# Two weighted sums in the choice of experts: each list laid out four times over by ScalarE ahead of the product

## The chip, the core and the metric

One Trainium2 chip, one of its cores. The time is what the device takes for one execution of the whole kernel, in microseconds; shown is the median of several executions.

## What is computed

One layer of a network for two groups of tokens, 128 of a prompt and 1024 latent ones, with a width of 1024. After two token mixers (a gated one and a recurrent one) comes a channel mixer that picks, for each token and each of 8 heads, 16 out of 16384 small experts. This part of the reference matters here:

```python
v1, i1 = lax.top_k(s[:, :, 0], PEER_TOPK)
v2, i2 = lax.top_k(s[:, :, 1], PEER_TOPK)
cand = (v1[..., :, None] + v2[..., None, :]).reshape(n_tok, PEER_HEADS, PEER_TOPK * PEER_TOPK)
cand_idx = (i1[..., :, None] * N_KEYS + i2[..., None, :]).reshape(...)
top_v, top_j = lax.top_k(cand, PEER_TOPK)
idx = jnp.take_along_axis(cand_idx, top_j, axis=-1).reshape(n_tok, PEER_HEADS * PEER_TOPK)
g = jax.nn.softmax(top_v, axis=-1)
```

Two lists of 128 keys are scored, the best 16 of each are kept, the 256 sums of pairs are searched for the best 16, and the pair of key indices behind each winner names its expert. Each token's output is the sum, over its 128 experts, of gelu(x . u) g v.

## The kernel before

Tokens lie on the partitions, 128 to a tile; tile 0 is the prompt, tiles 1 to 8 the latent tokens. The kernel goes through the prompt, then through the recurrent mixer of all latent tiles, then through the group of tiles 5 to 8 (GA), then that of tiles 1 to 4 (GB), each with its weights read as units of 512 KB. A unit is split by `split` (lines 98 to 100) into a rounded part, which ScalarE copies (line 99), and a rest, which VectorE subtracts (line 100); TensorE multiplies with both (`mmx`, lines 124 to 131). The experts are then applied in two ways. For tiles 4 to 8 (`DENSE`) a table G of gates is built with one-hot products (`build_G`, lines 515 to 560) and a loop over all 128 blocks of 128 experts (lines 1055 to 1081) multiplies everything: this is the dense loop, which takes the second half of the time. For tiles 0 to 3 (`GATHER`) the rows of the chosen experts are fetched one by one by GpSimd's indirect DMAs, and VectorE does the dot products and the sums (`gather`, lines 792 to 827).

The choice for a tile is `combine` (lines 422 to 513). `top16` has left the best 16 values `tv` and indices `ti` of both key lists. Of the 256 sums only 50 can be among the best 16; they are written to `cand` (lines 434 to 440), and `top16` finds the best 16 of each head among them (lines 443 to 446), values in `cv`, places in `cp`. `itf` and `pf` are the indices and places in half precision. The place is turned into two key indices without a lookup: `cmp_` compares each place with the starts of the 16 rows of sums (line 466), `di` holds the differences of neighbouring indices of the first list (lines 468 and 469), and the sum over `cmp_` times `di` is the index (line 470 and `tree`, lines 461 to 465). A second such sum, with the lengths of the rows (line 476), gives the place within the row, and a third, a comparison for equality (line 481) times the indices of the second list (line 482), gives the second index. Each product has 8 heads x 16 x 16 = 2048 elements a partition in half precision, winner innermost: in lines 470 and 482 the second factor has one value of the list for each run of 16 (`lp`, line 458), in line 476 it is a constant table that lies in full. Line 488 is an exponential on ScalarE, for the gates.

`combine` is a generator: each `yield` is a place where other work may come between. It runs for tile 0 ahead of the latent tokens, for tiles 5 to 8 while GB's first units are worked on (`choose_q`, advanced by `tick` with the rates of line 34 and 642), for tile 4 in two halves of four heads each at the end of GB (lines 736 to 741 and 763), and for tiles 1 to 3 inside the dense loop (`combine_late`, lines 767 to 782, advanced by `fill`, line 1013), where its lists lie in row buffers and VectorE's instructions are recorded under line 119. The order of each engine's instructions is fixed when the program is built, by a planner that takes the program's order as priority and estimated durations; at run time each engine does its instructions in that order and waits for others by semaphores.

Of the kernel before, what the change touches and what calls it, by code (L numbers as in the profile page):

```python
# [11 lines left out]
F16 = mybir.dt.float16  # L12
# [3 lines left out]
AF = mybir.ActivationFunctionType  # L16
OP = mybir.AluOpType
# [19 lines left out]
NC_ = 50  # L37
# [14 lines left out]
def hybrid_kernel(ctx, tc, x_all, pos, c2t, w_ada, b_ada, wst, wspt, bsp, lbraw, vecs, fng, skt, state,  # L52
                  ut, urow, vrow, masks, ident_d, small, y_p, y_s, ns):
    nc = tc.nc
    V, A, P, G = nc.vector, nc.scalar, nc.tensor, nc.gpsimd
# [366 lines left out]
    def combine(gp, t, tv, ti, al=None, c4=None, V=V, h0=0, h1=8, res=None):  # L422

        if al is None:
            def al(name, n, dt=F32):
                return gp.tile([128, n], dt, name=name, bufs=1)

            def c4(name):
                return gp.tile([128, 2048], F16, name=name, tag="c4", bufs=3)
        h8 = lambda x: x.rearrange("p (a b) -> p a b", a=8)[:, 0:nh]  # L430
        nh = h1 - h0
        tv, ti = tv[:, h0:h1], ti[:, h0:h1]
        hs = slice(h0 * 16, h1 * 16)
        cand = h8(al("cand", 8 * NC_))
        for i in range(8):
            n = LENS[i]
            V.tensor_tensor(out=cand[:, :, OFFS[i]:OFFS[i] + n], in0=tv[:, :, 1, 0:n],
                            in1=tv[:, :, 0, i:i + 1].to_broadcast([128, nh, n]), op=OP.add)
        V.tensor_tensor(out=cand[:, :, 42:50], in0=tv[:, :, 0, 8:16],
                        in1=tv[:, :, 1, 0:1].to_broadcast([128, nh, 8]), op=OP.add)  # L440
# [7 lines left out]
        itf = al("itf", 256, F16).rearrange("p (a b c) -> p a b c", a=8, b=2)[:, 0:nh]  # L448
# [6 lines left out]
        cmp_, prod = [c4(n).rearrange("p (a b c) -> p a b c", a=8, b=16)[:, 0:nh] for n in ("cmp", "prod")]  # L455
        SH = [128, nh, 16, 16]
        hk = lambda x: x[:, :, None, :].to_broadcast(SH)
        lp = lambda x: x[:, :, :, None].to_broadcast(SH)
        cst = lambda x: x[:, None].to_broadcast(SH)

        def tree(dst):
            for n in (8, 4, 2):
# [4 lines left out]
        di = h8(al("di", 128, F16))  # L467
        V.tensor_tensor(out=di[:, :, 0:15], in0=itf[:, :, 0, 1:16], in1=itf[:, :, 0, 0:15], op=OP.subtract)
        V.memset(di[:, :, 15:16], 0.0)
        V.tensor_tensor(out=prod, in0=cmp_, in1=lp(di), op=OP.mult)  # L470
        yield
        tree(r3(res[:, 0]))
        V.tensor_tensor(out=r3(res[:, 0]), in0=r3(res[:, 0]),
                        in1=itf[:, :, 0, 0:1].to_broadcast([128, nh, 16]), op=OP.add)
# [4 lines left out]
        V.tensor_tensor(out=pf, in0=pf, in1=ro, op=OP.subtract)  # L479
        yield  # L480
        V.tensor_tensor(out=cmp_, in0=hk(pf), in1=cst(C["cj"]), op=OP.is_equal)
        V.tensor_tensor(out=prod, in0=cmp_, in1=lp(itf[:, :, 1, :]), op=OP.mult)
        yield
        tree(r3(res[:, 1]))

# [76 lines left out]
    def group(gp, tiles, hpar, native):  # L562
# [172 lines left out]
        for b in range(16):  # L735
            if b == 8:
                for i in split_at:
                    res = gp.tile([128, 384], F32, name="res", bufs=1).rearrange("p (a b) -> p a b", a=3)
                    halves[i] = res
                    choose_q.append(combine(gp, tiles[i], tv[i], ti[i], h1=4, res=res))  # L740
                    rate["choose"] = 1.5
            w = unit(u + 44 + b, native)
            skb = gp.tile([128, 128], F32, name="skb", bufs=2)
            nc.sync.dma_start(skb, skt[:, b, :])
            ps = pmm("pq")
            projT(ps[:, :T], w, opd_q)
            qs = h512("qs")
            A.activation(qs[:, :T], ps[:, :T], AF.Copy)
            pss = ptp("psc")
            for i in range(n):  # L750
                P.matmul(pss[:, i * 128:(i + 1) * 128], qs[:, i * 128:(i + 1) * 128], skb, start=True, stop=True)
            for i in range(n):
                top16(gp, pss[:, i * 128:(i + 1) * 128], tv[i][:, b // 2, b % 2, :], ti[i][:, b // 2, b % 2, :], 128)
        rate["gather"] = before
        for i in range(n):
            t = tiles[i]
            if tiles is GB and t in GATHER:

                for z, x in enumerate((tv[i], ti[i].bitcast(F32))):
                    nc.sync.dma_start(tvi_d[t][:, z * 256:(z + 1) * 256], x.rearrange("p a b c -> p (a b c)"))  # L760
                late.append(t)
            elif i in halves:
                choose_q.append(combine(gp, t, tv[i], ti[i], h0=4, res=halves[i]))
            else:
                choose_q.append(combine(gp, t, tv[i], ti[i]))
# [289 lines left out]
    for e in range(129):  # L1055
        if e < 128:
# [6 lines left out]
            if e < 2:  # L1063
                a = early[e]
            else:
                a = dp.tile([128, TD], F32, name="a", bufs=2)
# [127 lines left out]
```

## Time and profile before

| | us |
|---|---|
| median of 3 runs | 3648.53 (3641.53 to 3650.37) |
| the profiled execution's own time | 3648.09 |
| its span, from the first to the last instruction | 3646.3 |
| TensorE, VectorE, ScalarE, GpSimd busy | 3339.6, 2834.4, 1109.9, 1432.2 |

PE is TensorE, PEld its weight loads, DVE VectorE, ACT ScalarE, POOL GpSimd, SP the engine that issues most DMAs. L99 is line 99 of the kernel before. A row such as `prod<-cmp,di 128x2048` names what is written and what is read; what stands in brackets is how long the engine sat idle ahead of the instruction, and what it waited for. The dense loop starts at about 1740 us and ends some 20 us before the span does.

### The profile page before, as it was taken

Reading aid. Unit: us, or ns where it says so; the run is one execution under the profiler, and the core shown is the slowest. Engines: PE = TensorE matmul, PEld = TensorE weight load, DVE = VectorE, ACT = ScalarE, POOL = GpSimd, SP = SyncE. Lnnn points to the kernel's source line nnn. Section 1 sums busy time; section 2 is a strip of 40 time slices with the busy share of each in tenths; the row PEclk is TensorE's granted clock in tenths of the full one; section 3 lists DMA queues with packets and bytes.
Section 4 is the critical chain, followed back from the end, with each engine's and each line's share of the span. In section 5 each row is a group of like instructions: output and inputs, shape, how many; then the busy total and the mean of one; then the engine's idle time right before and its main releaser. Section 6 shows DMA issues by size and latency. Waiting matters only on the chain. (4 is left out here: it accounts for less than half of the span.)

```text
span 3646.3 us, 48811 instructions
## 1 busy us (share of the span) xinstructions
PE 3339.6 (92%) x17547; PEld 2765.2 (76%) x17547; DVE 2834.4 (78%) x5427; ACT 1109.9 (30%) x2075; POOL 1432.2 (39%) x1128
## 2 busy tenths in 40 slices
PE   8888999899888899877789999989999989999997
PEld 4375888675666676566788988888898878898996
DVE  2316668786799888697787889888888888788887
ACT  2511343320323565625222222222222222222222
POOL 0102101654112323200365564655555466555654
PEclk9899999999989999999899999999999999999998
DMA  8787323799533778742898998899989799989986
GB/s 286 281 294 248 117 89 106 260 316 346 178 121 122 254 288 312 246 155 107 274 331 307 321 325 281 309 316 327 322 316 321 257 331 337 328 304 318 335 320 248
DMA packets 361956, 971.12 MB, mean 266 GB/s; under 512 B 32720, under 2 KB 142672, under 8 KB 356080
## 3 DMA queue, kind: packets, MB, share of 16 engines
q0 software_dynamic: 149824, 546.37, 42.3%
q1 hardware_dynamic: 211888, 421.62, 33.6%
q8 instruction: 138, 2.26, 0.3%
q14 instruction: 106, 0.87, 0.1%
HBM read 897.07 MB, written 70.80 MB: 265 GB/s over the span
## 5 line engine op out<-in xcount | busy, mean ns | idle before, releaser
L802 POOL DMA_INDIRECT gu<-in_urow_dram,ix x512 | 692.4, 1352 | 1039.5 <-DVE jk L805 465.3
L815 POOL DMA_INDIRECT gv<-in_vrow_dram,ix x512 | 685.4, 1339 | 783.1 <-DVE acc L820 384.5
L805 DVE SCALAR_TENSOR_TENSOR jk<-gu,h2r 128x1024 f16<-128x1024 f32 x512 | 625.5, 1222 | 139.1 <-DMA gu<-in_urow_dram,ix 132.4
L820 DVE SCALAR_TENSOR_TENSOR acc<-gv,act,acc 128x1024 f32<-128x1024 f32 x508 | 651.3, 1282 | 37.7 <-DMA gv<-in_vrow_dram,ix 30.1
L129 PE MATMUL pH<-h2DH,uH 128*128 128x320 f32 x2016 | 625.7, 310 | 10.9 <-DVE accd L1052 10.2
L131 PE MATMUL pH<-h2DH,uL 128*128 128x320 f32 x2016 | 623.4, 309 | 3.4 <-DVE uL L100 3.4
L130 PE MATMUL pH<-h2DL,uH 128*128 128x320 f32 x2016 | 623.8, 309 | 0.0
L129 PEld LDWEIGHTS pH<-h2DH,uH 128*128 128x128 f32 x2016 | 380.2, 189 | 21.0 <-DVE accd L1052 14.9
L130 PEld LDWEIGHTS pH<-h2DL,uH 128*128 128x128 f32 x2016 | 380.0, 188 | 4.5
L131 PEld LDWEIGHTS pH<-h2DH,uL 128*128 128x128 f32 x2016 | 379.8, 188 | 4.4 <-DVE uL L100 4.4
L129 PE MATMUL pout<-vH,aH 128*128 128x512 f32 x768 | 298.6, 393 | 23.3 <-ACT vH L99 16.1
L130 PE MATMUL pout<-vL,aH 128*128 128x512 f32 x768 | 300.2, 391 | 5.3 <-DVE vL L100 5.3
L99 ACT ACTIVATE vH<-vr 128x1024 fp32r<-128x1024 f32 x128 | 133.4, 1058 | 556.1 <-DMA vr<-in_vrow_dram 280.9
L131 PE MATMUL pout<-vH,aL 128*128 128x512 f32 x768 | 299.9, 391 | 1.4 <-DVE aL L100 1.3
L129 PE MATMUL prot<-vH,aH 128*128 128x512 f32 x512 | 210.2, 411 | 54.4 <-DVE accd L1052 48.3
L99 ACT ACTIVATE wH<-wraw 128x1024 fp32r<-128x1024 f32 x118 | 124.8, 1059 | 435.1 <-PE pq L130 160.1
L100 DVE TENSOR_TENSOR vL<-vr,vH 128x1024 fp32r<-128x1024 f32 x128 | 156.2, 1221 | 86.5 <-ACT vH L99 86.4
L130 PE MATMUL prot<-vL,aH 128*128 128x512 f32 x512 | 206.9, 404 | 0.0
L99 ACT ACTIVATE uH<-ur 128x1024 fp32r<-128x1024 f32 x126 | 133.4, 1059 | 241.3 <-PE pH L130 228.4
L131 PE MATMUL prot<-vH,aL 128*128 128x512 f32 x512 | 206.3, 403 | 0.0
L551 PE MATMUL pG<-oh 128*128 128x128 f16 x1280 | 177.1, 315 | 29.8 <-ACT sqj L255 12.6
L551 PEld LDWEIGHTS <-oh 128*128 128x128 f16 x1280 | 146.0, 130 | 75.8 <-issue 57.4
(343 smaller groups left out, 6279.8 us busy)
## 6 DMA issues: line engine op xcount, KB each, us to landing
wraw<-in_wst_dram SPq DMA_DIRECT2D x216, 512.0 KB, 5.3
vr<-in_vrow_dram SPq DMA_DIRECT2D x128, 512.0 KB, 6.5
ur<-in_ut_dram SPq DMA_DIRECT2D x126, 512.0 KB, 6.5
G_d<-Gs SPq DMA_DIRECT2D x40, 1024.0 KB, 5.1
Gt<-G_d SPq DMA_DIRECT2D x160, 256.0 KB, 10.0
wraw<-in_w_ada_dram SPq DMA_DIRECT2D x48, 512.0 KB, 5.1
gu<-in_urow_dram,ix POOLq DMA_INDIRECT x512, 6.6
gv<-in_vrow_dram,ix POOLq DMA_INDIRECT x512, 6.7
```

The lines of the kernel that those rows point to most:

```text
L99: A.activation(H, src, AF.Copy)
L100: return V.tensor_tensor(out=L, in0=src, in1=H.bitcast(F32), op=OP.subtract)
L129: P.matmul(ps, a[0], b[0], start=first, stop=False)
L130: P.matmul(ps, a[0], b[1], start=False, stop=False)
L131: P.matmul(ps, a[1], b[0], start=False, stop=last)
L551: P.matmul(pg[:, :, tt], oh[:, 0, :, tt], og[a][:, :, tt], start=(a == 0), stop=(a == 1))
L802: G.indirect_dma_start(out=ur, out_offset=None, in_=urow, in_offset=bass.IndirectOffsetOnAxis(ap=ix[:, c:c + 1], axis=0))
L805: paced(V.scalar_tensor_tensor(jk, ur, 1.0, h2r, op0=OP.mult, op1=OP.mult, accum_out=dots[:, k:k + 1]))
L815: G.indirect_dma_start(out=vr, out_offset=None, in_=vrow, in_offset=bass.IndirectOffsetOnAxis(ap=ix[:, c:c + 1], axis=0))
L820: paced(V.scalar_tensor_tensor(acc, vr, act[:, k:k + 1], acc, op0=OP.mult, op1=OP.add))
```

## The change

Ahead of the two products with a list, ScalarE writes each value of the list four times side by side into the columns of `cand`, which nothing reads any more by then (`weigh`). The product reads `cmp_` and `prod` as runs of four, and the second factor as rows of four equal values, each row four times over. The values are the same. The product with the lengths and the trees stay.

```diff
--- before.py
+++ after.py
@@ -431,7 +431,8 @@
         nh = h1 - h0
         tv, ti = tv[:, h0:h1], ti[:, h0:h1]
         hs = slice(h0 * 16, h1 * 16)
-        cand = h8(al("cand", 8 * NC_))
+        cand_ = al("cand", 8 * NC_)
+        cand = h8(cand_)
         for i in range(8):
             n = LENS[i]
             V.tensor_tensor(out=cand[:, :, OFFS[i]:OFFS[i] + n], in0=tv[:, :, 1, 0:n],
@@ -455,7 +456,15 @@
         cmp_, prod = [c4(n).rearrange("p (a b c) -> p a b c", a=8, b=16)[:, 0:nh] for n in ("cmp", "prod")]
         SH = [128, nh, 16, 16]
         hk = lambda x: x[:, :, None, :].to_broadcast(SH)
-        lp = lambda x: x[:, :, :, None].to_broadcast(SH)
+
+        def weigh(x):
+
+            x4 = cand_.bitcast(F16)[:, 0:nh * 64].rearrange("p (a b c) -> p a b c", a=nh, c=4)
+            A.activation(x4, x[:, :, :, None].to_broadcast([128, nh, 16, 4]), AF.Copy)
+            f4 = lambda y: y.rearrange("p a b (c d) -> p (a b) c d", d=4)
+            V.tensor_tensor(out=f4(prod), in0=f4(cmp_),
+                            in1=x4.rearrange("p a b c -> p (a b) c")[:, :, None].to_broadcast([128, nh * 16, 4, 4]),
+                            op=OP.mult)
         cst = lambda x: x[:, None].to_broadcast(SH)
 
         def tree(dst):
@@ -467,7 +476,7 @@
         di = h8(al("di", 128, F16))
         V.tensor_tensor(out=di[:, :, 0:15], in0=itf[:, :, 0, 1:16], in1=itf[:, :, 0, 0:15], op=OP.subtract)
         V.memset(di[:, :, 15:16], 0.0)
-        V.tensor_tensor(out=prod, in0=cmp_, in1=lp(di), op=OP.mult)
+        weigh(di)
         yield
         tree(r3(res[:, 0]))
         V.tensor_tensor(out=r3(res[:, 0]), in0=r3(res[:, 0]),
@@ -479,7 +488,7 @@
         V.tensor_tensor(out=pf, in0=pf, in1=ro, op=OP.subtract)
         yield
         V.tensor_tensor(out=cmp_, in0=hk(pf), in1=cst(C["cj"]), op=OP.is_equal)
-        V.tensor_tensor(out=prod, in0=cmp_, in1=lp(itf[:, :, 1, :]), op=OP.mult)
+        weigh(itf[:, :, 1, :])
         yield
         tree(r3(res[:, 1]))
```

## Rows read from the trace of the kernel before

**Rows 1.** The page: busy time, share of the span and instructions of each engine.

```profile
PE 3339.6 (92%) x17547; PEld 2765.2 (76%) x17547; DVE 2834.4 (78%) x5427; ACT 1109.9 (30%) x2075; POOL 1432.2 (39%) x1128
```

**Rows 2.** Busy time by stretch: us, then each engine's busy us (instructions), PEclk, DMA.

```profile
1055.00:1205.00 150.00, 119.89 (x471) 87.64 (x470) 143.28 (x477) 47.32 (x84) 31.09 (x26) 0.87 0.38 122
1600.00:1665.00 65.00, 44.83 (x202) 35.29 (x200) 56.78 (x272) 14.27 (x19) 0.88 (x2) 0.87 0.23 76
2200.00:2600.00 400.00, 375.36 (x2058) 338.61 (x2057) 337.58 (x484) 97.39 (x141) 222.28 (x165) 0.97 0.89 313
```

**Rows 3.** Timeline of TensorE: start us, us, instruction, [idle before and its releaser].

```profile
308.08 1.20 PE L129 MATMUL prow<-wH,hTAH 128*128 128x512 f32 x4 [2.10 <-ACT wH L99]
...
313.85 0.79 PE L130 MATMUL prow<-wL,hTAH 128*128 128x512 f32 x1 [4.57 <-DVE wL L100]
...
1078.24 0.51 PE L129 MATMUL prow<-wH,hTBrH 128*128 128x512 f32 x1 [2.40 <-DVE th L593]
...
1157.88 0.50 PE L131 MATMUL pzab<-hTBrH,wL 128*128 128x512 f32 x1 [2.12 <-DVE wL L100]
...
1171.75 0.79 PE L131 MATMUL pzab<-hTBrH,wL 128*128 128x512 f32 x1 [5.25 <-DVE wL L100]
...
1613.25 0.79 PE L131 MATMUL pq<-h2H,wL 128*128 128x512 f32 x1 [10.68 <-DVE wL L100]
...
1642.53 0.80 PE L131 MATMUL pq<-h2H,wL 128*128 128x512 f32 x1 [7.19 <-DVE wL L100]
...
1683.71 0.52 PE L505 MATMUL pidx<-ident,res 128*128 128x128 f32 x3 [3.12 <-DVE res L465]
```

**Rows 4.** Products of the choice: count, duration ns min/median/max, first and last start, forms.

```profile
L470 DVE TENSOR_TENSOR prod<-cmp,di x7: 1214/2280/2285, 308.4 to 1675.4; 128x2048 f16<-128x2048 f16 x5, 128x1024 f16<-128x1024 f16 x2
...
L482 DVE TENSOR_TENSOR prod<-cmp,itf x7: 1206/2283/2292, 323.6 to 1681.0; 128x2048 f16<-128x2048 f16 x5, 128x1024 f16<-128x1024 f16 x2
...
L119 DVE TENSOR_TENSOR prod<-cmp,late x6: 2281/2282/2286, 1754.2 to 2910.8; 128x2048 f16<-128x2048 f16 x6
...
L476 DVE TENSOR_TENSOR prod<-cmp,cs x7: 678/1217/1221, 313.9 to 1678.1; 128x2048 f16<-128x2048 f16 x5, 128x1024 f16<-128x1024 f16 x2
```

**Rows 5.** Line 533, a product that multiplies by rows of four.

```profile
L533 DVE TENSOR_TENSOR oh<-oh,gl x160: 407/418/473, 1182.6 to 1725.2; 128x512 f16<-128x512 f16 x160
```

**Rows 6.** ScalarE's groups by shape: count, busy us, mean ns, idle before.

```profile
L99 ACT ACTIVATE h2H<-full 128x512 fp32r<-128x512 f32 x16 | 9.7, 630 | 0.3
...
L312 ACT ACTIVATE K<-F 128x128 f32<-128x128 f32 x8 | 2.5, 311 | 0.3
```

**Rows 7.** Line 488, the exponential: its instructions, its waits, who waited for it.

```profile
L488 ACT ACTIVATE ex<-ex x7: 258/310/311, 306.8 to 1675.3; 128x128 f32<-128x128 f32 x5, 128x64 f32<-128x64 f32 x2
L488 ACT ACTIVATE late<-late x3: 310/311/312, 1756.7 to 2909.5; 128x128 f32<-128x128 f32 x3
...
  DVE ex L487: 47.7, 5
...
  DVE late L119: 9.1, 2
...
  ACT wH L99: 4.4, 1
```

**Rows 8.** Timeline of VectorE in the last half choice.

```profile
1675.38 1.22 DVE L470 TENSOR_TENSOR prod<-cmp,di 128x1024 f16<-128x1024 f16 x1
...
1681.04 1.23 DVE L482 TENSOR_TENSOR prod<-cmp,itf 128x1024 f16<-128x1024 f16 x1
```

**Rows 9.** Timeline of ScalarE at the same place.

```profile
1675.34 0.26 ACT L488 ACTIVATE ex<-ex 128x64 f32<-128x64 f32 x1
```

**Rows 10.** Timeline of VectorE at the dense loop's first product.

```profile
1740.01 1.56 DVE L1069 TENSOR_TENSOR a<-a,Gt 128x640 f32<-128x640 f32 x2 [13.91 <-DMA Gt<-G_d]
```

**Rows 11.** Waits from 1740 to 3620 us: us in total, times, longest.

```profile
ACT vH L99 <- PE prot L131: 275.0, 32, 14.3
...
PE prot L129 <- DVE accd L1052: 48.3, 15, 9.6
```

## The prediction, made before the result was known

> **What bounds the kernel now.** I read the busy times first. TensorE is busy 92% of the span and VectorE 78% [rows 1], so over the whole kernel it is TensorE's work that fills the time. The product that the change touches is VectorE work, and an average can't say whether VectorE holds TensorE up where that product lies; so I went to the stretches next. All twenty products lie in five places: one choice of experts ahead of the latent tokens (tile 0), four while the second latent group begins (tiles 5 to 8), two halves at that group's end (tile 4), and three inside the dense loop (tiles 1 to 3). From 1055 to 1205 us VectorE is busy 143.3 of 150 us and TensorE 119.9; from 1600 to 1665 us it is 56.8 of 65 against 44.8. In the dense loop (2200 to 2600 us as its sample) it is the other way: TensorE 375 of 400, VectorE 338 [rows 2]. So VectorE bounds the two earlier stretches, and TensorE the loop.
>
> The order of TensorE's instructions shows the same from the other side. It stops for VectorE 4.57 us at 313.85, 2.40 at 1078.24, 2.12 at 1157.88, 5.25 at 1171.75, 10.68 at 1613.25, 7.19 at 1642.53 and 3.12 at 1683.71 [rows 3]; each time a list product stands among the instructions just ahead on VectorE. These seven stops are where the change can pay.
>
> **What an edit costs or saves.** A product with the list spread along its innermost step takes 2.28 us for 2048 elements (five by each of two lines, and six in the dense loop) and 1.21 for 1024 (two by each line). The product with the lengths, same shape and type, where the second factor lies in rows, takes 1.217 and 0.678 [rows 4]. After the change the second factor has rows of four equal values, each row read four times. Such a pattern is in the trace already: the one-hot products multiply by rows of four, and 512 elements take 0.418 us [rows 5], on the line through 0.678 at 1024 and 1.217 at 2048 (0.53 ns an element: 0.678 less 512 x 0.53 is 0.41). I therefore take 1.217 and 0.678: 1.06 us saved by each of 16 whole products, 0.53 by each of four half ones, in all 17.0 + 2.1 = 19.1 us of VectorE.
>
> The added copies write 512 elements each (256 for a half). ScalarE copies 512 in 0.630 us and 128 in 0.311 [rows 6], so 256 is 0.630 - 256 x 0.83 ns = 0.42. That is 16 x 0.63 + 4 x 0.42 = 11.8 us more on an engine that is busy 30% [rows 1]; as work it costs nothing. As a hop it may cost: VectorE now waits for ScalarE ahead of each product, and ScalarE for VectorE ahead of each copy.
>
> The nearest row for such a hop is the exponential of the same choice, which goes VectorE, ScalarE, VectorE ten times. VectorE never waits for it by the trace. ScalarE sat idle for its input 47.7 us in five of the seven earlier ones and 9.1 us in two in the dense loop, and one weight split that stood behind it started late by 4.4 us [rows 7]. That split is the one TensorE waits 2.10 us for at 308.08 [rows 3]. So ten hops cost TensorE 2.1 us, or 0.21 each. The bounds for one copy are nothing (nine of the ten) and 2.1 (the tenth); I take the mean, 0.21, thus 20 x 0.21 = 4.2 us.
>
> For the second copy of a choice the list has long been there; it only has to wait until the first product has read the shared columns, which ends 4.4 us ahead of the second even in a half choice (1675.38 + 1.22 to 1681.04 [rows 8]). For the first, the list of differences is ready just ahead of the comparison, and the comparison covers the copy, unless ScalarE is taken. It is taken in one place where nothing else fills VectorE: in the last half, ScalarE ends its exponential at 1675.34 + 0.26 = 1675.60 [rows 9], a copy behind that would end at 1676.02, and the product stood at 1675.38 [rows 8]: 0.64 us late. The ends here are nothing (the copy goes ahead of the exponential) and 1.9 (it goes behind the 1.28 us table load, too).
>
> The copy's place is the candidate list, so the next choice's candidates can't be written until the second product is done. Some candidate sums that now run ahead of that product move behind it. VectorE is fed throughout there [rows 2], so this changes an order, not a sum. No DMA, no SP or POOL instruction is added or moved.
>
> **The sum.** Tile 0: the first product stands ahead of the 4.57 us stop, 1.06. Tile 5: both products ahead of the stop of 2.40, 2.13. Tile 6: the next wait of TensorE names ScalarE's evacuation, nothing. Tile 7: both ahead of the stop of 2.12, so that much. Tile 8: the first ahead of 5.25, 1.06; the second has no stop behind it. First half of tile 4: one product ahead of 10.68, one ahead of 7.19, 2 x 0.53 = 1.06. Last half: it is a chain that ends in the table for the dense loop, whose first product waits 13.91 us for its data [rows 10]; 1.06 again. Together 8.5. The three choices in the dense loop save 6.4 us of VectorE, but there ScalarE's splits wait for TensorE (275 us in 32 waits, up to 14.3) and TensorE's wait for VectorE is 48.3 us of the 1880 from 1740 us on [rows 11]; I take nothing, with 0 and 6.4 as ends. So 8.5 - 0.64 - 4.2 = 3.7 us less. The profiled execution took 3648.09 us, its span 3646.3 and 1.8 around it; it would come to 3644.4. The median of the runs is 3648.53, 0.44 above it, so I say **3645 us**. About 0.3% (11 us) is what a measurement can tell from no change; this lies within it.
>
> A rule speaks for less. The Trainium skill, "Perfetto Trace Analysis", section "Identifying the Most-Contended Engine", says to work first on the engine with the highest occupancy; by that rule alone, with VectorE not the busiest, the sum of gains would be zero and the time 3648.5. Its next section allows for stretches with different leaders, and the two VectorE-bound stretches of this trace are such.
>
> **The rivals.**
> *The whole saving arrives.* VectorE may matter in the dense loop too, since gathers and additions fill what it has left, and a choice that ends sooner starts its gathers sooner. For it: 48.3 us of TensorE's waits there name VectorE [rows 11]. Against it: TensorE is busy 94% of that stretch [rows 2]. All 19.1 us: 3629.4.
> *Hidden after all.* Each shortened stop is taken up by the next late thing, the weight split's own start on ScalarE, which waits for TensorE's buffers: 3648.5. For it, TensorE's 92% [rows 1].
> *The copy holds up ScalarE (slower).* ScalarE takes its instructions in a fixed order. Where VectorE runs late against that order, a copy waits for it, and the weight split or gelu behind the copy waits too, and TensorE with it, as at 308.08. The place is the two VectorE-bound stretches and the dense loop; the price is up to 2.1 us a copy; it decides from 7.9 / 20 = 0.39 us a copy on. If half of the twenty cost 2.1: 21 - 7.9 = 13 us more, 3662. Against it: one such case among ten exponentials [rows 7].
> The Trainium skill, "ScalarE: Activation LUTs", section "Rules for kernel authors", would leave simple arithmetic on VectorE; that is this rival's side, and the ten exponentials of the trace do not bear out a loss.
> *The product keeps its old pace.* If rows of four, each read four times, don't run as fast as rows of four from one list, only the hops remain: 4.2 + 0.64, 3653. Against it: the one-hot row [rows 5].
>
> **How the numbers follow.** Forecast 0.45; hidden 0.13; old pace 0.04: these are within 0.3%, 0.62. The whole saving, or so much of it that 11 us are passed, 0.25. ScalarE held up, 0.13. The range reaches from the whole saving, 3629, to 3658, which takes in the old pace (3653) and copies at about 0.9 us each (20 x 0.9 - 7.9 = 10 more); left out are the dearer end of the held ScalarE and the last of the fast side, under 2 in 10.
>
> **What would show it.** Right: the two products at about 1.22 and 0.68 us, twenty copies of 0.63 or 0.42 us on ScalarE, VectorE's busy time lower by some 19 us, the stops at 313.85, 1078, 1157, 1171, 1613 and 1642 shorter by about a microsecond each, and the dense loop as long as before. Wrong: products still at 2.28; VectorE with idle time ahead of the products that names the copy; ScalarE idle ahead of the copies with splits late behind them; or a dense loop that is shorter or longer by more than some microseconds, which would say that the new order of instructions, not the price of the product, moved the time.

## The result, and the profile after

The changed kernel takes **3629.44 us** (median of 7 runs, 3623.6 to 3636.22), the kernel before, run beside it, 3649.33 (median of 7, 3640.72 to 3657.56): a ratio of 0.9945, 95% interval 0.9931 to 0.9959, so 15 to 25 us less, 20 in the middle. The prediction said 3645, with a range from 3629 to 3658. The time lies 0.4 us inside the fast end, where the rival "the whole saving arrives" (3629.4) stood. The profiled execution took 3629.96 us, with a span of 3628.2.

The first view is the page's busy times, to be held against [rows 1].

```profile
PE 3336.8 (92%) x17547; PEld 2764.3 (76%) x17547; DVE 2817.6 (78%) x5427; ACT 1121.3 (31%) x2095; POOL 1429.2 (39%) x1128
```

VectorE has as many instructions as before and is busy 16.8 us less (2834.4 - 2817.6; instructions overlap a little, and an overlap counts once), ScalarE has twenty more and is busy 11.4 us more. The shares have not moved: at this height nothing shows that 20 us are gone.

The products, by their tile (count, duration in ns as minimum, median and maximum, first and last start, forms), answer [rows 4]:

```profile
L465 DVE TENSOR_TENSOR prod<-cmp,cand x14: 680/1213/1226, 306.5 to 1668.3; 128x2048 f16<-128x2048 f16 x10, 128x1024 f16<-128x1024 f16 x4
...
L119 DVE TENSOR_TENSOR prod<-cmp,late x6: 1216/1218/1225, 1740.2 to 2898.0; 128x2048 f16<-128x2048 f16 x6
```

All twenty are at the pace of the product with the lengths, 1.21 and 0.68 us. So the products take less by what was worked out, 16 x 1.06 + 4 x 0.53 = 19.1 us. The copies answer [rows 6, 7]. The view has the line's instructions, what ScalarE waited for ahead of them, and last who waited for them:

```profile
L463 ACT ACTIVATE cand<-di x7: 416/629/630, 304.6 to 1662.1; 128x512 f16<-128x512 f16 x5, 128x256 f16<-128x256 f16 x2
...
  DVE di L477: 25.5, 4
  DVE prod L465: 23.1, 5
...
who waited for it (us, times):
```

0.63 and 0.42 us, as taken. ScalarE sits idle ahead of them for VectorE, as it did ahead of the exponential. Under "who waited for it" stands nothing: no wait of VectorE is put down to a copy, and the most that it sits idle ahead of a list product is 0.10 us (0.03 before), ahead of each of the two in the last half. That half shows why; first VectorE's, then ScalarE's timeline there, answering [rows 8, 9]:

```profile
1662.31 0.69 DVE L475 TENSOR_TENSOR cmp<-pf,cs 128x1024 f16<-128x1024 f16 x1
1663.11 0.69 DVE L465 TENSOR_TENSOR prod<-cmp,cand 128x1024 f16<-128x1024 f16 x1
...
1668.30 0.69 DVE L465 TENSOR_TENSOR prod<-cmp,cand 128x1024 f16<-128x1024 f16 x1
```

```profile
1662.08 0.42 ACT L463 ACTIVATE cand<-di 128x256 f16<-128x256 f16 x1 [0.38 <-DVE di L477]
1662.51 1.28 ACT L497 ACT_TABLE_LOAD   x1
1663.80 0.26 ACT L497 ACTIVATE ex<-ex 128x64 f32<-128x64 f32 x1
```

The copy goes ahead of the table load and the exponential, and ends at 1662.50, half a microsecond before the comparison that covers it. The 0.64 us of the prediction stood for the other order.

Where did the 20 us go? I cut both traces at the same instructions of TensorE: its first product with the mixer's first unit after the prompt (A, 308.1 us before), its first product with the second latent group's input (B, 1043.1), the first product of the dense loop's hidden layer (C, 1664.9), the first of the loop's rotating blocks (D, 1785.9) and the last (E, 3623.5). The view is busy time by stretch, as in [rows 2] (us, then each engine's busy us with its instructions, PEclk, DMA); from B to C and from D to E, first before, then after.

```profile
1043.10:1664.90 621.80, 537.71 (x2589) 395.32 (x2588) 539.95 (x1604) 276.50 (x680) 140.82 (x119) 0.93 0.60 211
1785.90:3623.50 1837.60, 1758.03 (x9673) 1587.00 (x9671) 1543.75 (x2015) 445.46 (x652) 1044.21 (x770) 0.98 0.90 315
```

```profile
1037.20:1652.60 615.40, 531.90 (x2590) 392.79 (x2588) 531.16 (x1604) 282.68 (x690) 140.42 (x119) 0.94 0.60 213
1771.90:3605.40 1833.50, 1757.46 (x9673) 1587.22 (x9671) 1538.81 (x2013) 447.84 (x656) 1042.80 (x769) 0.98 0.90 315
```

From B to C (tiles 5 to 8 and the first half of tile 4: 9.6 us saved on VectorE) the stretch is 6.4 us shorter. In this pair TensorE is idle almost as long as before (621.80 - 537.71 = 84.1, 615.40 - 531.90 = 83.5) and busy 5.8 us less for the same products, at a mean granted clock of 0.94 instead of 0.93, that is with less of its time at the lower of its two levels (1.2 and 2.4 GHz). More executions of the two orders, named below, divide it otherwise: idle 84.1 to 87.5 us before and 81.3 to 83.5 after, busy 535.5 to 537.7 and 531.9 to 533.3, so about half from each. From D to E the loop is 4.1 us shorter. Only the four products of tiles 2 and 3 lie there (4.3 us saved); tile 1's two lie between C and D, at 1754.2 and 1769.6 us before. Over the fixed stretches of [rows 2] the same is seen less clearly, since the work has moved by 6 to 18 us under them:

```profile
1055.00:1205.00 150.00, 125.03 (x530) 93.60 (x530) 141.69 (x461) 59.76 (x113) 30.47 (x29) 0.92 0.43 145
...
2200.00:2600.00 400.00, 377.37 (x2089) 341.40 (x2088) 335.47 (x484) 99.33 (x146) 219.74 (x164) 0.97 0.88 310
```

TensorE gets 530 products done in the first where it did 471, and 2089 for 2058 in the second.

The stops of TensorE answer [rows 3] (start, us, instruction, idle before and releaser):

```profile
307.84 2.08 PE L129 MATMUL prow<-wH,hTAH 128*128 128x512 f32 x4 [3.68 <-ACT wH L99]
310.93 0.80 PE L130 MATMUL prow<-wL,hTAH 128*128 128x512 f32 x1 [1.01 <-DVE wL L100]
...
1056.35 0.79 PE L130 MATMUL prow<-wL,hTBrH 128*128 128x512 f32 x1 [5.94 <-DVE wL L100]
...
1155.13 0.50 PE L131 MATMUL pzab<-hTBrH,wL 128*128 128x512 f32 x1 [2.86 <-DVE wL L100]
...
1600.67 0.79 PE L131 MATMUL pq<-h2H,wL 128*128 128x512 f32 x1 [10.14 <-DVE wL L100]
...
1629.71 0.80 PE L131 MATMUL pq<-h2H,wL 128*128 128x512 f32 x1 [6.66 <-DVE wL L100]
```

The two of the half choice are shorter by half a microsecond each, 10.68 to 10.14 and 7.19 to 6.66: in this pair, one half product apiece. Between 1050 and 1180 us none can be paired with one of [rows 3], because the planner has laid the order out anew (about 240 of VectorE's 2577 instructions ahead of the loop stand elsewhere, and about 110 of the 1692 in it).

At 308 the stop for ScalarE is 1.6 us longer and the next 3.6 shorter. What that comes to is read from an instruction ahead of both, the making of the differences `di`, before the first copy. First before, then after; VectorE's row, then ScalarE's:

```profile
306.19 0.21 DVE L468 TENSOR_TENSOR di<-itf 128x120 f16<-128x120 f16 x1
290.32 1.28 ACT L488 ACT_TABLE_LOAD   x1
306.77 0.31 ACT L488 ACTIVATE ex<-ex 128x128 f32<-128x128 f32 x1 [15.16 <-DVE ex L487]
306.99 1.99 ACT L99 ACTIVATE wH<-wraw 128x1024 fp32r<-128x1024 f32 x2
```

```profile
304.34 0.21 DVE L477 TENSOR_TENSOR di<-itf 128x120 f16<-128x120 f16 x1
304.59 0.63 ACT L463 ACTIVATE cand<-di 128x512 f16<-128x512 f16 x1 [15.38 <-DVE di L477]
305.24 1.28 ACT L497 ACT_TABLE_LOAD   x1
306.53 0.31 ACT L497 ACTIVATE ex<-ex 128x128 f32<-128x128 f32 x1
306.75 1.04 ACT L99 ACTIVATE wH<-wraw 128x1024 fp32r<-128x1024 f32 x1
```

The copy has a price here. The table load, which stood in ScalarE's idle time at 290.32, now stands behind the copy, and so do the exponential and the weight split `wH`. From the end of `di` to TensorE's product with `wH` it was 308.08 - 306.40 = 1.68 us and is 307.84 - 304.55 = 3.29, 1.6 us more. All six kernels in which ScalarE copies tile 0's list have the load there and the 1.6 us; the seven in which nothing copies it have neither. But the next stop waits for VectorE's `wL`, and to its end it was 313.85 - 306.40 = 7.45 and is 310.93 - 304.55 = 6.38: 1.07 less, one product. What the copy took, the next stop gave back.

The loop's first product waits 13.87 us for its table [rows 10]; and the waits from there on, against [rows 11], are hardly different:

```profile
ACT vH L99 <- PE prot L131: 268.2, 30, 12.9
...
PE prot L129 <- DVE accd L1061: 50.1, 13, 9.4
```

### The profile page after: what moved, and what is told of

It reads as the page before. It is cut to its first block, busy times and chain, and to the rows that moved or that the text cites. A ratio compares the mean times of both kernels' runs of the same rounds, so it can differ in the third digit from the quotient of the medians.

```text
span 3628.2 us, 48825 instructions
## 1 busy us (share of the span) xinstructions
PE 3336.8 (92%) x17547; PEld 2764.3 (76%) x17547; DVE 2817.6 (78%) x5427; ACT 1121.3 (31%) x2095; POOL 1429.2 (39%) x1128
## 5 line engine op out<-in xcount | busy, mean ns | idle before, releaser
L129 PE MATMUL pout<-vH,aH 128*128 128x512 f32 x768 | 300.6, 394 | 21.9 <-ACT vH L99 16.1
L129 PE MATMUL prot<-vH,aH 128*128 128x512 f32 x512 | 209.2, 409 | 54.4 <-DVE accd L1061 50.1
L99 ACT ACTIVATE aH<-a 128x640 fp32r<-128x640 f32 x128 | 94.2, 737 | 358.3 <-DVE a L1078 352.2
```

What stands on the lines that cost most here:

```text
L99: A.activation(H, src, AF.Copy)
L129: P.matmul(ps, a[0], b[0], start=first, stop=False)
```

## The experiments

### The parts alone

Each of the first four kernels keeps the copies in one place only; elsewhere the old product stands.

```diff
         def weigh(x):
+            if not (t == 0):
+                V.tensor_tensor(out=prod, in0=cmp_, in1=x[:, :, :, None].to_broadcast(SH), op=OP.mult)
+                return
```

This is for tile 0; the others have `t in GA`, `t == 4` and `t in (1, 2, 3)`.

> Only tile 0's choice has the copies; all other choices multiply as before. Chain theory (the choice of tile 0 is what the gathers wait for; VectorE's gather products stand ahead of weight splits and wait for rows, so an earlier start takes away the stops at 353 and 365 us and the half-clock stretches behind them): 7 to 11 us less than before. Saving theory (each place gives what its products save of VectorE): 2.1 us less. Order theory (the gain comes from how the whole program is laid out anew): nothing that fits either, and the parts do not add up to 20.

> Only the four choices of tiles 5 to 8 have the copies. Chain theory: 3 to 6 us less, since VectorE holds TensorE up in that stretch. Saving theory: 8.5 us less. Order theory: anything.

> Only the two half choices of tile 4 have the copies. Chain theory and saving theory: 1 to 2 us less, not to be told from no change. Order theory: several us either way.

> Only the three choices in the dense loop have the copies. Chain theory: 0 to 3 us less, since TensorE is the fuller engine there. Saving theory: 6.4 us less. Order theory: several us either way.

Measured against 3651.79 us (median of 35):

| copies in | us | ratio (95%) | less by |
|---|---|---|---|
| tile 0 | 3646.57 | 0.9994 (0.9983 to 1.0005) | 5.2 |
| tiles 5 to 8 | 3650.69 | 1.0000 (0.9987 to 1.0013) | 1.1 |
| the halves of tile 4 | 3648.88 | 0.9995 (0.9981 to 1.0009) | 2.9 |
| tiles 1 to 3, in the loop | 3641.85 | 0.9973 (0.9960 to 0.9986) | 9.9 |

The four differences add up to 19.1 us, the whole to 19.9; each has an interval of some 4 or 5 us to either side, so this sum rules little out. Only the loop's part is clear of nothing by itself, with 5.1 to 14.6 us, and it is the one to which the prediction gave nothing. No theory fits all four. The chain theory misses tile 0 (7 to 11 us asked, at most 6.2 by the interval) and the loop (0 to 3). The saving theory misses tiles 5 to 8, its largest part: 8.5 us asked, at most 4.7 by the interval.

### Who copies, and what the copy alone costs

VectorE makes the copies itself (first edit); ScalarE makes them, but the product reads only the first of the four, at the old pace (second edit).

```diff
-            A.activation(x4, x[:, :, :, None].to_broadcast([128, nh, 16, 4]), AF.Copy)
+            V.tensor_copy(x4, x[:, :, :, None].to_broadcast([128, nh, 16, 4]))
```

```diff
-            V.tensor_tensor(out=f4(prod), in0=f4(cmp_),
-                            in1=x4.rearrange("p a b c -> p (a b) c")[:, :, None].to_broadcast([128, nh * 16, 4, 4]),
-                            op=OP.mult)
+            V.tensor_tensor(out=prod, in0=cmp_, in1=x4[:, :, :, 0:1].to_broadcast(SH), op=OP.mult)
```

> The copies are made by VectorE in place of ScalarE, the products read them as in the changed kernel. Work theory (time follows VectorE's own work in the places of the choice, and a hop to ScalarE costs nothing): twenty copies of 512 or 256 half-precision elements come back onto VectorE, 0.3 to 0.6 us each, 6 to 11 us of it, so 10 to 14 us less than before. Hop theory (the hop costs what was forecast, 0.24 us each): about as fast as the changed kernel or faster, 17 us less or more.

> ScalarE lays the lists out as in the changed kernel and the products wait for that, but the products read only the first of the four copies, one value for sixteen elements, so they keep the old 2.28 us. Work theory: no different from before, within 4 us. Hop theory: 4 to 5 us more than before. Order theory (the gain comes from the new order alone): clearly less than before.

The first took 3646.7 us against 3651.78 (0.9994, 0.9980 to 1.0007), at most 7.3 us less, and so misses both theories; the second 3674.29 (1.0068, 1.0052 to 1.0084), which none of its three theories had. Their lines, in this order, and the second one's stretch from B to C:

```profile
L463 DVE COPY cand<-di x7: 284/420/424, 304.3 to 1663.7; 128x512 f16<-128x512 f16 x5, 128x256 f16<-128x256 f16 x2
```

```profile
L464 DVE TENSOR_TENSOR prod<-cmp,cand x14: 1214/2284/2293, 308.9 to 1691.7; 128x2048 f16<-128x2048 f16 x10, 128x1024 f16<-128x1024 f16 x4
...
1044.10:1675.50 631.40, 535.88 (x2590) 394.34 (x2588) 539.61 (x1604) 281.60 (x690) 139.54 (x119) 0.94 0.57 207
```

With the old pace and the copies the kernel is some 23 us slower than before though VectorE has no more to do (539.61 us from B to C, 539.95 before). 9.6 of it lie from B to C, 9.3 from D to E (1846.9 us). Read by itself that is a price of more than 1 us a copy, and the reason to look at the hop again.

### Thinning out the loop's choices

`LATE` says how fast the choice is advanced in the loop. Its second number at 0.4, in the kernel before and in the changed one:

```diff
-LATE = (3, 0.8)
+LATE = (3, 0.4)
```

> The kernel before, with the choices in the dense loop spread over twice as many blocks (0.4 in place of 0.8 steps at a time for the second and third). Burst theory (a choice in the loop packs VectorE so that the evacuations of TensorE's banks come late; what counts there is how dense the burst is): 4 to 8 us less than before without any change of the product. Work theory: no change, since VectorE's work is the same.

> The changed kernel with the same spreading. Burst theory: 2 to 5 us less than the changed kernel's 3629, so 22 to 25 us less than before. Work theory: as the changed kernel, 20 us less than before.

Against 3651.78 they took 3672.63 us (1.0063, 1.0049 to 1.0077) and 3652.60 (1.0003, 0.9992 to 1.0014). The first is 20.9 us dearer than with 0.8, the second 20.7 (0.8 above before, where the changed kernel stands 19.9 below). That a choice spread out would disturb the loop less, falls, and so does the work theory, by which neither kernel would have moved; but the change keeps its 20 us at either setting (3672.63 - 3652.60 = 20.0).

### More work, the same work, another order

The last four ask what a microsecond of VectorE is worth, and what a new order alone does. Half of each old product is made once more in the kernel before; each new product is made twice in the changed one; `LATE` goes to 1.6 in the changed one; `LEAD` goes from 60 to 66 in the one before, which starts the loop's choices a little sooner. The first edit, made alike on the product with the second list:

```diff
-        V.tensor_tensor(out=prod, in0=cmp_, in1=lp(di), op=OP.mult)
+        for k in range(nh // 2, nh + 1, nh // 2):
+            V.tensor_tensor(out=prod[:, 0:k], in0=cmp_[:, 0:k], in1=lp(di)[:, 0:k], op=OP.mult)
```

> The kernel before, in which each of the twenty products with a list is made on its first half once more ahead of the whole one: by the rows for 1024 and 512 elements 16 x 1.21 + 4 x 0.68 = 22.1 us more of VectorE, with no copy and no ScalarE in the way. If VectorE's time in a choice counts about one for one (work), about 22 us more than before, ratio 1.006. If it counts more than twice, as the run with copies and the old pace against the changed kernel would have it (45 us between them for 19.1 us of VectorE), about 50 us more, 1.014. If that run was dear because of the hop through ScalarE (hop), this one shows the plain price of the work, 20 us or less. If the times come from the new order that each program is given (layout), anything from 0 to 40.

> The changed kernel with each of the twenty products made twice: 2 x 1.22 us instead of 2.28 in the kernel before, copies and waits as in the changed one, so VectorE has as much to do as in the run with copies and the old pace (16 x 0.16 + 4 x 0.15, some 3 us more). Hop: as that run, 25 us above before, 1.007. Work: 3 us above before, 1.001, and some 22 above the changed kernel. Layout: apart from that run by 10 us or more though the work is the same.

> The changed kernel with the second number of LATE at 1.6 instead of 0.8: the choices in the dense loop are taken in steps twice as dense, the opposite of the two runs with 0.4, which cost 21 and 23 us. Buffers (a choice in the loop takes two row buffers from the gathers as long as it runs, so a shorter one gives them back sooner): 8 to 20 us below the changed kernel. Burst (dense steps crowd out the evacuations and the weight splits on VectorE): 5 to 20 us above it. Neither: within 4 us of it.

> The kernel before with LEAD at 66 instead of 60: the choices in the dense loop begin six gathered rows sooner, and nothing else is asked of any engine; the planner lays the loop out anew. Work, hop and buffers: the time of before, within 4 us (0.999 to 1.001). Layout: 5 to 15 us away from it, either way; what comes out is the size of the scatter that has to be allowed for in every other run of this study.

Measured against 3651.33 us (median of 28):

| kernel | us | ratio (95%) | against its parent |
|---|---|---|---|
| before, half products added | 3673.27 | 1.0057 (1.0040 to 1.0074) | +21.9 for 22.1 us of VectorE |
| changed, products twice | 3663.43 | 1.0030 (1.0018 to 1.0043) | +32.0 for 22.2 us of VectorE |
| changed, LATE at 1.6 | 3640.04 | 0.9970 (0.9961 to 0.9979) | +8.6, same work |
| before, LEAD at 66 | 3659.39 | 1.0019 (1.0008 to 1.0031) | +8.1, same work |

(The changed kernel, as a parent, is put 19.9 us below before.) The first is the cleanest: no copy, no ScalarE, only work, and as a whole it counts about one for one (14.6 to 27 us by the interval), though its program has an order of its own, too. Here are its stretches B to C and D to E.

```profile
1047.20:1680.40 633.20, 538.80 (x2590) 396.48 (x2588) 550.54 (x1614) 276.81 (x680) 141.93 (x119) 0.92 0.57 207
1803.30:3648.70 1845.40, 1759.75 (x9673) 1588.98 (x9671) 1545.98 (x2018) 446.78 (x652) 1051.57 (x773) 0.98 0.89 314
```

B to C is 11.4 us longer for 11.1 us of work (8 x 1.21 + 2 x 0.68), C to D 1.9 (122.9 us) for 3.8 (2 x 0.68 + 2 x 1.21), D to E 7.8 for 4.8 (4 x 1.21). So it is one for one in the first, and not stage by stage: D to E took 1835.1 to 1843.8 us in executions of one order, which is more than the difference.

The second tells against a price of the hop, though it misses the work theory's 3 us as well. Its copies and waits are those of the kernel at the old pace, and VectorE has as much to do; yet it is 12.1 us above before and not 22.5, and from B to C it takes 624.4 us, not 631.4:

```profile
1040.00:1664.40 624.40, 535.93 (x2590) 394.63 (x2588) 540.77 (x1614) 281.42 (x690) 140.53 (x119) 0.93 0.58 210
1785.80:3636.60 1850.80, 1762.90 (x9673) 1589.62 (x9671) 1542.89 (x2017) 448.12 (x656) 1042.82 (x770) 0.98 0.89 312
```

624.4 is 2.6 us above before for 1.5 us more work in ten products. What it is late by stands in the loop: 1850.8 us.

With `LATE` at 1.6 the changed kernel lost 8.6 us, after it had lost 20.7 at 0.4. A theory that wants the choice short (row buffers given back sooner) and one that wants it thin (bursts) would each have one of the two go the other way; neither holds, and 0.8 is the best of the three.

The last tells how much an order alone does, and it is what the layout theory had, 5 to 15 us. Ahead of the loop VectorE's instructions stand as before, one for one; in the loop about 165 stand elsewhere, none is added:

```profile
1786.50:3636.80 1850.30, 1765.95 (x9673) 1590.39 (x9671) 1543.84 (x2015) 445.98 (x652) 1038.90 (x770) 0.98 0.89 313
```

1850.3 against 1837.6, with VectorE's 1543.8 us unchanged.

### All traces, cut at the same places

Where two kernels share a program in a stretch, their traces can be put together. Ahead of the loop the kernel before, the one with copies in the loop alone, and those with `LEAD` at 66 and `LATE` at 0.4 have one order of VectorE's instructions; so do the changed kernel and its two with another `LATE`. In the loop the kernel before shares its order with the three that have copies ahead of the loop alone, and the changed one with the one that has them in the loop alone. Each cell is from such traces, and is worked out from the starts of the instructions A to E; the first row starts at the end of tile 0's `di`, since A itself is moved by the copy, as shown above.

| stretch | order of before, us | order of the changed, us | difference | saved on VectorE |
|---|---|---|---|---|
| `di` to B (tile 0) | 736.7, 733.8, 737.2, 732.4 | 732.6, 737.6, 731.7 | -1.1 | 2.1 |
| B to C (tiles 5 to 8, half of 4) | 621.8, 624.8, 622.3, 621.4 | 615.4, 614.7, 614.5 | -7.7 | 9.6 |
| C to D (last half of 4, tile 1) | 121.0, 121.1, 121.0, 121.1 | 119.3, 119.3, 119.4 | -1.7 | 3.2 |
| D to E (tiles 2 and 3) | 1837.6, 1835.1, 1843.8, 1837.5 | 1833.5, 1834.3 | -4.6 | 4.3 |

Together -15.1 us of 19.1 by the traces, and 19.9 (15 to 25) by the clocks of the runs. In B to C and C to D the two columns are clear of each other; in `di` to B they overlap, and in D to E 0.8 us lie between them. Tile 1's part gave nothing from C to D: with the copies in the loop alone it is 121.1 us, with those of the halves alone 119.3. From B to C the order moves the time as well as the work: the copies of tiles 5 to 8 alone, in almost the order of the changed kernel, gave 619.1 us, 3.5 less than the mean of before for 8.5 us of work.

Single stops are far steadier than stretches. Each is given, from unrounded starts, for all kernels whose product there has the old pace and no copy, for those that have the change there, and for the one with copies and the old pace:

| place | before | changed | copies, old pace | one product |
|---|---|---|---|---|
| tile 0, end of `di` to the product with `wL` | 7.43 to 7.44 (6 kernels) | 6.37 (4) | 7.44 | 1.06 |
| first half of tile 4, first stop | 10.68 to 10.69 (6) | 10.14 to 10.16 (4) | 10.69 | 0.53 |
| the same, second stop | 7.01 to 7.19 (6) | 6.66 to 6.68 (4) | 7.21 | 0.53 |
| last half, end of `di` to the transposes `pidx` | 9.33 (6) | 8.40 to 8.41 (4) | 9.47 | 2 x 0.53 |

The rows of the kernel with copies and the old pace, and the transposes of the changed one, against [rows 3]:

```profile
306.71 0.21 DVE L474 TENSOR_TENSOR di<-itf 128x120 f16<-128x120 f16 x1
314.36 0.80 PE L130 MATMUL prow<-wL,hTAH 128*128 128x512 f32 x1 [2.08 <-DVE wL L100]
1623.65 0.79 PE L131 MATMUL pq<-h2H,wL 128*128 128x512 f32 x1 [10.69 <-DVE wL L100]
1652.96 0.80 PE L131 MATMUL pq<-h2H,wL 128*128 128x512 f32 x1 [7.21 <-DVE wL L100]
```

```profile
1670.44 0.52 PE L514 MATMUL pidx<-ident,res 128*128 128x128 f32 x3 [2.18 <-DVE res L474]
```

At these places the cause is shown: the stop ends sooner by about what the faster product saves (the second by 0.33 to 0.53), and the copy alone costs 0.0 to 0.2 us.

## Why the prediction was right, and where its size was wrong

**Right.** The pace of the products, the copies' cost and place, the 19.1 us that the products save, the way it went, and the stops at tile 0 and tile 4: 1.07 us for 1.06, then 0.53 and 0.33 to 0.53 for 0.53 each, and 0.93 for 1.06 in the last half. The products at 1.218 us stand beside 2.283 before. The Trainium skill, "VectorE: DVE Perf Modes", section "Side-by-side: where the cycles go for N=2048 bf16", has 1224 and 2293 ns for the two paces; these traces, in f16, agree to within 6 and 10 ns. The two rivals with no gain (hidden after all; the product at its old pace) are out, and so is the one with a loss: the copy did hold up ScalarE at 308 us, but the next stop took it up.

**Luck.** The range was met by 0.4 us. The forecast of 3.7 us less was a fifth of what came, and the whole saving had a chance of 0.25. That the total equals the work saved is in part luck, too: the traces give 15.1 us, and orders without any work saved moved the kernel by 8 to 21.

**Wrong: two terms of the sum, both to the same side.**

*"I take nothing, with 0 and 6.4 as ends"* for the dense loop. The loop's part alone gave 9.9 us (5.1 to 14.6) by the runs, and 4.6 from D to E by the traces. So the loop was not as long as before. How much of this is the product's price and how much the new order is not shown: the prediction's own sign for "the new order, not the price" was a loop that is shorter or longer by more than some microseconds, and that is what came. The step that misled was the sample of 400 us [rows 2], with TensorE at 94% and VectorE at 84%: it averages one choice with long stretches between choices. As I read it, and this is not shown, work in a choice delays the weight splits and the emptying of TensorE's accumulators that stand behind it in VectorE's fixed order; TensorE's 48.3 us of waits for `accd` [rows 11] were the row that said so, but they are 50.1 after. They were quoted for the rival and then set aside.

The rule by which the gain would have been zero was read by TensorE's matmul share, 92%. The same section of the Trainium skill ("Perfetto Trace Analysis", "Identifying the Most-Contended Engine") says that for TensorE this share is no good measure, and names instead the share of peak work and that of its weight loads. The weight loads are 76% here, beside VectorE's 78% [rows 1]. Read so, the rule does not put VectorE behind TensorE, and these runs do not speak against it.

*"20 x 0.21 = 4.2 us"* for the hops, and 0.64 for the last half. The price at one place was there, 1.6 us at 308 by the copy and the table load behind it, and within the bounds of 0 and 2.1; but it was hidden by the next stop, and the kernel with copies and the old pace shows 0.0 to 0.2 us at the stops of the table. The one wait behind an exponential at 308 was a single event, and dividing it over ten hops and then charging it to twenty, without asking which stop comes next, made a cost out of it. The kernel in which VectorE copies is 5.1 us faster than before, the change 19.9. The row that the prediction named from the Trainium skill, "ScalarE: Activation LUTs", section "Rules for kernel authors", gives relu, max, min, add and mul to VectorE; a copy is not among them, so it does not decide here. Copying costs VectorE 0.42 us each, some 7.9 us, and the rest of the gap goes with its loop, with 1846.0 us another order again.

*"Together 8.5"* for the stages ahead of the loop, before those deductions, was about right: 10.5 by the traces (1.1 + 7.7 + 1.7). What is over lies in tiles 5 to 8, where the order changed too. The last half's 1.7 stands against 1.06; after the transposes, which come 0.93 sooner, the way to the loop's first product is 0.7 us shorter as well.

So 3.7 us was 8.5 - 0.64 - 4.2 + 0, and measured is about 10.5 - 0 - 0 + 5 to 10.

**What stays open.** How the loop's gain, and that from tiles 5 to 8, divide between the price of the product and the new order: no kernel here has the changed order with the old pace. Why copies with the old pace cost 23 us: it is not the hop as such, since the same hops with the product made twice cost 10 less. Ahead of the loop about 490 of its VectorE instructions stand elsewhere than before, the most of all kernels here; but that the order did it is argued, not shown. Nor is it shown why the orders of the loop in the two kernels compared here are among the shortest that were run: seven others, with no more work than before or 1 us of it, took 1843 to 1863 us against 1834 and 1838 (1843.8 in another execution of the order of before). With a scatter of 10 us between orders, the loop's share of the gain (4.6 or 9.9) can't be told closer. No version was faster than the changed kernel.

## What to carry to other kernels

Read the bound of an engine at the length of the piece of work that changes, not over a sample several times as long; where a fixed order runs through two engines, work on the less busy one can still count. Where a stop can be found in both traces, measure it, or measure to it from an instruction ahead of the change: here three of four such places repeated to 0.02 us over six kernels, while whole stretches scatter by 3 to 9 us. Before charging a hop between engines for a late instruction, ask whether the next stop waits for something later still. Where a planner lays the program out anew after any edit, measure first what an edit without work does (here 8 us, 0.2%, and 21 us at another pace of the choices), and take no difference smaller than that as the effect of the edit.

## What was not expected of the hardware

The same order of instructions does not take the same time in every execution: from tile 0's `di` to B it took 732.4 to 737.2 us over four executions of one order, and 731.7 to 737.6 over three of the other. A saving need not come back as idle time alone: from B to C about half of it came out of TensorE's busy time for the same products (535.5 to 537.7 us before, 531.9 to 533.3 after), at a mean granted clock of 0.94 instead of 0.93 in three of four executions. And one table load of 1.28 us, for the same work on ScalarE, can move from idle time into the way of a weight split when a copy is put ahead of it.
